# Shifting the slices of the transposed activations by 32 B each in a hybrid decoder layer

## The chip, the core and the metric

The kernel runs on one core of a Trainium2 chip. The metric is the device time of one execution in microseconds (us), median of the runs. The core's engines are called as in the profile: PE (TensorE, matmuls), PEld (its weight loads), DVE (VectorE), ACT (ScalarE), POOL (GpSimd) and SP (whose queue issues most transfers).

## The reference

One decoder layer on 256 tokens of 2048 features, all in float32. Two groups of attention heads share one input projection, one output projection follows, and then a gated feed-forward layer with a short causal convolution. Cut to what matters here:

```
h = rmsnorm(x, pre_mix_g)
proj = h @ w_in                       # 2048 -> 4368 columns: q, k, v of both groups, forget gates
o_a = sliding-window attention with sinks and ALiBi   (16 heads, 2 key/value heads)
o_b = forgetting attention with per-head gates        (16 heads)
x = x + rmsnorm(concat(rmsnorm(o_a), rmsnorm(o_b)) @ w_out, post_mix_g)
h = rmsnorm(x, pre_ffn_g)
u = causal_dwconv(h @ w_up)           # 2048 -> 11264 columns, width 3
gate, val = split(u)
x = x + rmsnorm((gelu(gate) * val) @ w_down, post_ffn_g)
```

## The kernel before

Every product is made from float32 operands that are split in two: a rounded high part and the rest, the low part. A product a*b is then taken as high*high + high*low + low*high. The tile hT holds the transposed normalised activations in this form: 16 slices (`kt`, one for each 128 of the 2048 features), and in each slice, for every one of 128 partitions, 256 high parts (one per token) and behind them 256 low parts, 512 float32 in all, which is 2048 B. The slices lie one behind the other, so that each begins at a multiple of 512 B. hT is filled from transposed x by ACT (high parts, L194) and DVE (low parts, L196) before the input projection, and a second time, as hT2, by L768 and L773 before the feed-forward layer. Then the same room serves once more, as `rest`, for some split weights of the last down projection.

Weights come in units of 1024 columns by SP's queue into `raw`, ACT rounds them into `whi`, and DVE writes the difference into `wlo` (L112 and L115). Where `still` is set, the low parts begin LOW = 56 elements, 224 B, into their buffer; whi and the unshifted wlo begin at multiples of 512 B.

The matmuls that read hT as the moving operand come in two kinds, with two output banks (m = 0, 1) for the two halves of 256 output columns:

```
pe.matmul(b, parts[u][0][:, a, m * P:(m + 1) * P], hT[:, kt, :], ...)                   # high
pe.matmul(b[:, 256:512], parts[u][1][:, a, m * P:(m + 1) * P], hT[:, kt, 0:256], ...)   # low
```

A high streams the 512 elements of a slice past 128 columns of whi, a low the first 256 past 128 columns of wlo. `proj_T4` (L284 and L290) serves the up projection: highs of slices 0 to 7 (16 matmuls), lows of 0 to 7, lows of 8 to 15, highs of 8 to 15, so that between groups of columns 32 highs or 32 lows follow each other. `proj_T` (L253 and L258) serves the queries and keys with stretches of 14 to 16, `unit_T` (L221 and L226) the first two groups, and `first_gate` (L928 and L932) the first columns of the up projection, half a slice at a time. In the value projection `mm3` (L309) uses hT the other way round: 128 elements of a slice are the weights, and 384 or 272 columns of whi and wlo stream.

PE's order is the order of the program text. The instructions of the other engines are ordered by a scheduler, except where the text fixes their order. Each matmul has a weight load of its own, which runs beside the matmul before it.

Matmuls that do not read hT: attention scores (L475), transposes of probabilities (L510), weighted sums (L522 to L536), output projection (`mm3` with oT), and the down projection (`product`, L967), where the weights are the moving operand and gated activations G or their sums are loaded.

The small tile gpre holds the gains of the first norm, 16 partitions of 512 B. It is loaded at L139 by ACT's queue, and read once, by the transpose at L175. The tile scr (tag "y") is scratch room for attention: rows and masks in its first 1280 columns, rotating scratch from column 1536 on, and from 1280 to 1536 the cumulated forget gates later on.

Of the kernel before, what the change touches and what calls it, by code (L numbers as in the profile page):

```python
# [8 lines left out]
F32 = mybir.dt.float32  # L9
F32R = mybir.dt.float32r  # L10
# [7 lines left out]
P = 128  # L18
S = 256
D = 2048  # L20
DFF = 5632
H = 16
KT = D // P
# [8 lines left out]
def hybrid_layer(ctx: ExitStack, tc: tile.TileContext, x, pre_mix_g, w_in, b_forget, sinks,  # L32
# [8 lines left out]
    const = ctx.enter_context(tc.tile_pool(name="const", bufs=1))  # L41
    main = ctx.enter_context(tc.tile_pool(name="main", bufs=1))
# [92 lines left out]
    const.tile([P, 120], F32, tag="room", name="room_c")  # L135
    small.tile([P, 112], F32, tag="room", bufs=1, name="room_s")

    gpre = const.tile([16, P], F32, tag="gpre", name="gpre")
    act.dma_start(gpre, pre_mix_g.rearrange("o (a p) -> (o a) p", p=P))  # L139
    x_in = main.tile([P, 2, D], F32, tag="x", name="x_in")  # L140
    xv = xf.rearrange("(t p) c -> p t c", p=P)

    first = [[], []]
# [1 line left out]
    for i in range(2):  # L145
        cs = slice(i * 256, (i + 1) * 256)
# [36 lines left out]
        pool.tensor_tensor(r, v, mhalf, op=ALU.pow)  # L183
        return r

    hT = main.tile([P, KT, 512], F32R, tag="hT", name="hT")
    def to_T(srcs, t0, n, g0, pin=False):

        for part in range(2):
            for kt, tb in srcs:  # L190
                hi = hT[:, kt, t0:t0 + n]
                gk = gcol[:, g0 + kt:g0 + kt + 1]
                if part == 0:
                    i = act.activation(hi, tb, AF.Copy, scale=gk)  # L194
                else:
                    i = dve.scalar_tensor_tensor(hT[:, kt, 256 + t0:256 + t0 + n], tb, gk,  # L196
                                                 hi.bitcast(F32), op0=ALU.mult, op1=ALU.subtract)
                if pin:
                    tc.keep_in_program_order(i)
# [115 lines left out]
    with tc.tile_pool(name="mixp", bufs=1) as mp:  # L315
# [30 lines left out]
                                   accum_out=sqx[t][:, c:c + 1]))  # L346


        scr = main.tile([P, 2 * D], F32, tag="y", name="scr")
        rowk, rowq, dist, u0, u1 = (scr[:, i * 256:(i + 1) * 256] for i in range(5))  # L350
        rot = [0]

# [278 lines left out]
        for p0, npair, cols in ((0, 3, 384), (3, 3, 384), (6, 2, 272)):  # L631
# [3 lines left out]
            for k0 in range(0, KT, per):  # L635
                na = min(per, KT - k0)
                hi, lo = w_unit(w_rows(w_in, k0, na, c0, cols), na, cols)
                for a in range(na):
                    kt = k0 + a
# [100 lines left out]
        out_half(1, evac_b, range(2))  # L740


        hT2 = main.tile([P, KT, 512], F32R, tag="hT", name="hT2")
        hT = hT2
        x_dram = tc.dram_tile([S, D], F32, name="x_dram")
        dffn, rmix = [], []
        sq2 = [small.tile([P, 4], F32, tag=f"sqm{t}", bufs=1, name=f"sqm{t}") for t in range(2)]
# [99 lines left out]
    with tc.tile_pool(name="ffn", bufs=1) as fp:  # L847
# [45 lines left out]
        def conv(b, ch, dst_tag):  # L893
            u = ubuf[cnt[0] % NU]
            cnt[0] += 1
            c = from_ring("cs")
            act.copy(c, b[:, 256:512])
            dve.tensor_tensor(u[:, 2:258], b[:, 0:256], c, op=ALU.add)  # L898
            pool.tensor_tensor(u[:, 2:258], u[:, 2:258], rowf, op=ALU.mult)  # L899
            y = from_ring(dst_tag)  # L900
            act.activation(y, u[:, 2:258], AF.Identity, bias=cw[:, 3, ch:ch + 1],  # L901
                           scale=cw[:, 2, ch:ch + 1])
            dve.scalar_tensor_tensor(y, u[:, 1:257], cw[:, 1, ch:ch + 1], y, op0=ALU.mult,  # L903
                                     op1=ALU.add)
            dve.scalar_tensor_tensor(y, u[:, 0:256], cw[:, 0, ch:ch + 1], y, op0=ALU.mult,
                                     op1=ALU.add)
            return y
# [141 lines left out]
        for half in range(2):  # L1049
# [4 lines left out]
            for g in range(FHALF // 2):  # L1054
# [11 lines left out]
                for m in range(2):  # L1066
                    y = conv(bg[m], c0 // P + m, "yg")
# [5 lines left out]
                for m in range(2):  # L1073
                    y = conv(bv[m], 44 + c0 // P + m, "yv")
# [90 lines left out]
        def rstd_y(t, n, v):  # L1165
            v2 = small.tile([P, 1], F32, tag="rv", name="rv")
            dve.scalar_tensor_tensor(v2, ysq[t][:, n:n + 1], 1.0 / D, v, op0=ALU.mult, op1=ALU.add)
            r = small.tile([P, 1], F32, tag="ry", bufs=2, name="ry")
            pool.tensor_tensor(r, v2, mhalf, op=ALU.pow)
            return r  # L1170
# [23 lines left out]
        r = rstd_y(0, 3, v)  # L1194
# [18 lines left out]
        r = rstd_y(1, 4, v)  # L1213
# [33 lines left out]
```

## Time and profile before

| | |
|---|---|
| median of 3 runs | 1064.84 us (1064.18 to 1065.08) |
| profiled execution, first to last instruction | 1062.6 us |
| instructions | 16272, of these 5890 matmuls |
| mean granted clock of TensorE | 0.996 |
| read from HBM | 201.68 MB, 194 GB/s over the span |

The profiled execution's own time is given as its span, from the first to the last instruction; the median of the runs lies 2.2 us above it. In the profile, L12 is line 12 of the kernel, `out<-in` are the program's names of what an instruction writes and reads, x counts instructions, and the records of successive matmuls overlap, so that the interval from one to the next is shorter than the duration of one. The chain of work is followed back from the last instruction, at each step to what released it.

### The profile page before, as it was taken

The numbers are of one execution on the slowest core, as the hardware profiler recorded it, in microseconds if no ns is written. First come the engines' busy times: TensorE is split into PE (matmuls) and PEld (weight loads), VectorE is DVE, ScalarE is ACT, GpSimd is POOL, SyncE is SP. The second block draws the span as 40 slices with busy tenths as digits, with TensorE's granted clock in tenths as the row PEclk, the third lists the DMA queues.
The fourth block names the chain that finished last, engine by engine and source line by source line (L and its number), as shares of the span: only waits on it lengthen the run. The fifth ranks groups of instructions, "written<-read, shape, count | busy, mean of one in ns | idle before, by whom it ended". The sixth has DMA issues, their size and how long they took to land.

```text
span 1062.6 us, 16272 instructions
## 1 busy us (share of the span) xinstructions
PE 1049.6 (99%) x5890; PEld 914.6 (86%) x5890; DVE 839.7 (79%) x1369; ACT 639.1 (60%) x1096; POOL 229.3 (22%) x256
## 2 busy tenths in 40 slices
PE   9999999999999999999999999999999999999996
PEld 7889988888889888888888888888888888888885
DVE  5988887887467887787767999668778687789987
ACT  6767667776556765566655556446556565556551
POOL 4253335441022121211212000002121121200004
PEclk9999999999999999999999999999999999999998
DMA  8745566555773876656665666666566665656563
GB/s 280 217 120 168 162 209 202 165 170 162 282 236 107 280 231 187 193 180 185 211 188 188 193 204 206 213 196 190 169 209 188 197 197 180 194 179 200 194 242 121
DMA packets 154285, 207.08 MB, mean 195 GB/s; under 512 B 6845, under 2 KB 131037, under 8 KB 153181
## 3 DMA queue, kind: packets, MB, share of 16 engines
q1 hardware_dynamic: 153200, 203.37, 60.7%
q10 hardware_dynamic: 1004, 2.68, 0.6%
q8 instruction: 46, 0.75, 0.3%
q14 instruction: 35, 0.28, 0.1%
HBM read 201.68 MB, written 4.21 MB: 194 GB/s over the span
## 4 chain that ended last, share of the span: by engine, by line
PE 84%; DVE 9%; issue 2%; DMA 2%; ACT 2%; POOL 1%; DVEq 0%; SPq 0%; POOLq 0%; ACTq 0%
PE bank_acc L284 15%; PE bank_att L284 14%; PE bank_acc L309 12%; PE bank_att L967 9%; PE bank_acc L290 8%; PE bank_att L290 7%; PE bank_acc L253 7%; DVE wlo L313 4%; PE bank_acc L258 4%; PE bank_acc L967 2%; PE bank_att L475 1%; PE bank_att L510 1%; DVE wlo L115 1%; PE bank_acc L932 1%; DMA raw<-in_w_down_dram 1%
## 5 line engine op out<-in xcount | busy, mean ns | idle before, releaser
L115 DVE TENSOR_TENSOR wlo<-raw,whi 128x1024 fp32r<-128x1024 f32 (+3 forms) x271 | 328.5, 1224 | 127.0 <-ACT whi L112 118.4
L112 ACT CAST whi<-raw 128x1024 fp32r<-128x1024 f32 (+3 forms) x270 | 273.2, 1029 | 131.8 <-issue 88.8
L899 POOL TENSOR_TENSOR room<-room,rowf 128x256 f32<-128x256 f32 x88 | 100.3, 1160 | 393.9 <-DVE room L898 392.0
L284 PE MATMUL bank_acc<-hT,whi 128*128 128x512 f32 x736 | 173.3, 390 | 0.0
L284 PEld LDWEIGHTS bank_acc<-hT,whi 128*128 128x128 f32 x736 | 136.4, 188 | 27.4
L967 PE MATMUL bank_att<-whi,G 128*128 128x512 f32 x488 | 156.0, 389 | 0.0
L284 PE MATMUL bank_att<-hT,whi 128*128 128x512 f32 x640 | 150.6, 390 | 0.0
L284 PEld LDWEIGHTS bank_att<-hT,whi 128*128 128x128 f32 x640 | 118.7, 188 | 23.9
L967 PEld LDWEIGHTS bank_att<-whi,G 128*128 128x128 f32 x488 | 91.6, 188 | 18.9
L967 PE MATMUL bank_att<-wlo,G 128*128 128x512 f32 x244 | 95.0, 389 | 0.2 <-DVE wlo L313 0.2
L290 PEld LDWEIGHTS bank_acc<-hT,wlo 128*128 128x128 f32 x736 | 89.3, 188 | 2.0
L290 PE MATMUL bank_acc<-hT,wlo 128*128 128x256 f32 x736 | 89.8, 279 | 0.0
L901 ACT ACTIVATE room<-room,cw 128x256 f32<-128x256 f32 x88 | 53.0, 602 | 60.6 <-POOL room L899 60.6
L253 PE MATMUL bank_acc<-hT,whi 128*128 128x512 f32 x352 | 88.0, 395 | 0.0
L309 PE MATMUL bank_acc<-whi,oT 128*128 128x512 f32 (+1 forms) x272 | 81.7, 379 | 0.0
L290 PEld LDWEIGHTS bank_att<-hT,wlo 128*128 128x128 f32 x640 | 77.6, 188 | 1.7
L290 PE MATMUL bank_att<-hT,wlo 128*128 128x256 f32 x640 | 77.9, 279 | 0.0
L903 DVE SCALAR_TENSOR_TENSOR room<-room,cw 128x256 f32<-128x256 f32 x88 | 62.4, 709 | 17.6 <-ACT room L901 17.3
L253 PEld LDWEIGHTS bank_acc<-hT,whi 128*128 128x128 f32 x352 | 63.3, 188 | 11.5
L313 DVE TENSOR_TENSOR wlo<-raw,whi 128x1024 fp32r<-128x1024 f32 (+1 forms) x56 | 61.3, 1119 | 12.1 <-ACT whi L312 12.1
L312 ACT CAST whi<-tb 128x1024 fp32r<-128x1024 f32 x42 | 44.0, 1050 | 43.0 <-PE bank_att L967 19.6
L312 ACT CAST whi<-raw 128x1024 fp32r<-128x1024 f32 (+1 forms) x56 | 52.3, 958 | 27.1 <-PE bank_att L967 20.6
(254 smaller groups left out, 1594.0 us busy)
## 6 DMA issues: line engine op xcount, KB each, us to landing
raw<-in_w_up_dram SPq DMA_DIRECT2D x176, 512.0 KB, 4.2
raw<-in_w_down_dram SPq DMA_DIRECT2D x58, 512.0 KB, 4.7
raw<-in_w_in_dram SPq DMA_DIRECT2D x51, 512.0 KB, 4.7
raw<-in_w_out_dram SPq DMA_DIRECT2D x32, 512.0 KB, 4.6
extra<-in_w_down_dram SPq DMA_DIRECT2D x20, 512.0 KB, 4.7
raw<-in_w_in_dram SPq DMA_DIRECT2D x16, 384.0 KB, 3.6
tb<-in_w_down_dram SPq DMA_DIRECT2D x10, 512.0 KB, 3.5
cb<-c_dram SPq DMA_DIRECT2D x8, 256.0 KB, 3.8
```

What stands on the lines that cost most here:

```text
L112: i1 = act.copy(hi[:, cs], raw[:, cs])
L115: i2 = dve.tensor_tensor(lo[:, cs], raw[:, cs], hi[:, cs].bitcast(F32), op=ALU.subtract)
L253: pe.matmul(b, parts[u][0][:, a, m * P:(m + 1) * P], hT[:, kt, :], start=(kt == 0), stop=(kt == KT - 1))
L284: pe.matmul(b, parts[u][0][:, a, m * P:(m + 1) * P], hT[:, kt, :], start=(kt == 0), stop=(kt == KT - 1))
L290: pe.matmul(b[:, 256:512], parts[u][1][:, a, m * P:(m + 1) * P], hT[:, kt, 0:256], start=False, stop=False)
L309: pe.matmul(b, a, r[:, cols], start=(first and i == 0), stop=(last and i == 2))
L312: act.copy(hi, src)
L313: dve.tensor_tensor(lo, src, hi.bitcast(F32), op=ALU.subtract)
L899: pool.tensor_tensor(u[:, 2:258], u[:, 2:258], rowf, op=ALU.mult)
L901: act.activation(y, u[:, 2:258], AF.Identity, bias=cw[:, 3, ch:ch + 1], scale=cw[:, 2, ch:ch + 1])
L903: dve.scalar_tensor_tensor(y, u[:, 1:257], cw[:, 1, ch:ch + 1], y, op0=ALU.mult, op1=ALU.add)
L967: pe.matmul(b[:, to] if to else b, a, r[:, cols], start=(first and i == 0), stop=(last and i == 2))
```

## The change

Slice k of hT now begins 512 + 8 elements, 2080 B, behind slice k - 1, so 32*k B past a multiple of 512. A class Rows stands for the tile and keeps the way in which the code indexes it. The tile grows by 512 B a partition; for that room gpre loses its own tile, and lies in scr[0:16, 1280:1408] instead. x_in, hT and scr are allocated earlier in the text, in the same order as before.

```
-    gpre = const.tile([16, P], F32, tag="gpre", name="gpre")
+    x_in = main.tile([P, 2, D], F32, tag="x", name="x_in")
+    SKEW = 8
+    class Rows:
+        def __init__(self, name):
+            self.t = main.tile([P, KT * (512 + SKEW)], F32R, tag="hT", name=name)
+        def __getitem__(self, at):
+            _, kt, cs = at
+            r = self.t[:, kt * (512 + SKEW):kt * (512 + SKEW) + 512]
+            return r[:, cs]
+    hT = Rows("hT")
+    scr = main.tile([P, 2 * D], F32, tag="y", name="scr")
+    gpre = scr[0:16, 1280:1408]
     act.dma_start(gpre, pre_mix_g.rearrange("o (a p) -> (o a) p", p=P))
-    x_in = main.tile([P, 2, D], F32, tag="x", name="x_in")
...
-    hT = main.tile([P, KT, 512], F32R, tag="hT", name="hT")
...
-        scr = main.tile([P, 2 * D], F32, tag="y", name="scr")
...
-        hT2 = main.tile([P, KT, 512], F32R, tag="hT", name="hT2")
-        hT = hT2
+        hT = Rows("hT2")
```

## The prediction

> **What bounds the kernel now.** I read the page first (busy shares, granted clock, the chain by line), then what TensorE waits for, then the chain of work in order of time, which gives the pace of each stretch of matmuls.
>
> ```profile
> PE 1049.6 (99%) x5890; PEld 914.6 (86%) x5890; DVE 839.7 (79%) x1369; ACT 639.1 (60%) x1096; POOL 229.3 (22%) x256
> PEclk9999999999999999999999999999999999999998
> PE 84%; DVE 9%; issue 2%; DMA 2%; ACT 2%; POOL 1%; DVEq 0%; SPq 0%; POOLq 0%; ACTq 0%
> ```
>
> TensorE is busy for 1049.6 of 1062.6 us, its granted clock is at the top digit until the last slice, and 84% of the chain is PE. The waits of PE are next; the columns are who waited for whom, us in total, times, longest us.
>
> ```profile
> PE bank_acc L169 <- DVE junk L164: 1.3, 1, 1.3
> PE bank_att L522 <- DVE pl L313: 0.5, 1, 0.5
> PE bank_acc L334 <- DMA x_in<-in_x_dram: 0.4, 1, 0.4
> PE bank_att L967 <- DVE wlo L313: 0.2, 1, 0.2
> ```
>
> These four are all that the view lists, 2.4 us together. So no other engine and no transfer holds PE up for long: whatever the change does to the interval from one matmul to the next goes straight into the time, and what it does on other engines does not, as long as they stay behind that little waiting. The matmuls that read hT are these (groups by line; after the count, busy us and mean ns of one record):
>
> ```profile
> L284 PE MATMUL bank_acc<-hT,whi 128*128 128x512 f32 x736 | 173.3, 390 | 0.0
> L284 PE MATMUL bank_att<-hT,whi 128*128 128x512 f32 x640 | 150.6, 390 | 0.0
> L290 PE MATMUL bank_acc<-hT,wlo 128*128 128x256 f32 x736 | 89.8, 279 | 0.0
> L290 PE MATMUL bank_att<-hT,wlo 128*128 128x256 f32 x640 | 77.9, 279 | 0.0
> L253 PE MATMUL bank_acc<-hT,whi 128*128 128x512 f32 x352 | 88.0, 395 | 0.0
> L258 PE MATMUL bank_acc<-hT,wlo 128*128 128x256 f32 x352 | 46.8, 281 | 0.0
> L309 PE MATMUL bank_acc<-whi,hT 128*128 128x384 f32 (+1 forms) x192 | 46.6, 322 | 0.0
> L309 PE MATMUL bank_acc<-wlo,hT 128*128 128x384 f32 (+1 forms) x96 | 30.6, 319 | 0.0
> ```
>
> That is 1376 + 352 = 1728 "highs" (512 columns of a slice, weights from whi), 1728 "lows" (256 columns, weights from wlo, which start 224 B past a multiple of 512), and 288 matmuls of the value projection, where hT is the weight and not the moving operand. The records overlap, so the 390 ns is no interval. The interval is read from the chain in order of time (start us, us, what, count):
>
> ```profile
> 455.55 7.29 PE bank_att L284 x32
> 462.84 3.73 PE bank_att L290 x32
> 466.57 3.65 PE bank_att L284 x16
> 470.22 3.63 PE bank_acc L284 x16
> ```
>
> A high takes 7.29/32 = 227.8 ns and a low 3.73/32 = 116.6 ns. The 16 highs just behind the lows take 3.65 us and the next 16 take 3.63. The timeline, cut at a start of such a stretch, shows why (start us, us from the first start to the last end):
>
> ```profile
> 521.51 1.32 PE L284 MATMUL bank_acc<-hT,whi 128*128 128x512 f32 x5
> 522.21 6.52 PE L284 MATMUL bank_acc<-hT,whi 128*128 128x512 f32 x28
> ```
>
> With 0.39 us for the last record, the first five highs start (1.32 - 0.39)/4 = 232.5 ns apart, the 28 from the fourth on (6.52 - 0.39)/27 = 227.0 ns. Nobody waits there: the same instruction on the same data layout is slow for some five matmuls after the switch from lows to highs, and then settles at 227 and stays. The pace is a steady state that has to be reached.
>
> **What the change does.** It adds and removes no instruction, semaphore or byte of transfer. It moves addresses: slice k of hT begins 2080 B behind slice k-1 instead of 2048, that is 32*k B past a multiple of 512. The weights do not move, so the distance (modulo 512 B) from the weights that are being loaded to the columns that stream past is no longer the same for all 16 slices, but goes round by 32 B a slice. In the loops a slice serves two matmuls (one per bank), so the distance changes at every second matmul. It also reads gpre from a corner of scr, and shifts what lies below hT by 512 B, which keeps its place modulo 512.
>
> The last part costs nothing:
>
> ```profile
> L139 ACTq DMA_DIRECT2D gpre<-in_pre_mix_g_dram x1: 458/458/458, 0.8 to 0.8; - x1
> L175 PE MATMUL bank_att<-ident,gpre x1: 283/283/283, 3.9 to 3.9; 16*128 16x16 f32 x1
> ```
>
> gpre is loaded at 0.8 us from ACT's queue and read once at 3.9 us, by L175. The columns of scr that it takes are written next by the cumulative sum of the forget gates, after the whole value projection; that stretch covers it, and without it one transpose of 0.283 us would be waited for. The writes of hT by ACT and DVE keep their shapes; at 32 B steps I put them at nothing too, since PE does not wait for ACT or DVE in the rows above beyond 0.7 us.
>
> What remains is what a changed distance does to an interval. The trace of before has three distances. Highs have distance 0 (slice and weights both at multiples of 512), lows 224. Two more stretches of the chain:
>
> ```profile
> 326.78 2.88 PE bank_acc L309 x24
> 234.61 0.69 PE bank_att L534 x3
> 235.31 0.36 PE bank_att L536 x3
> ```
>
> The 24 matmuls of 256 columns in the output projection have distance 0, and take 2.88/24 = 120.0 ns, against 116.6 for the lows: same width, no wait in either, other distance. So the distance matters, by 3.4 ns. The weighted sums L534 and L536 stream probabilities that lie 128 B past a multiple of 512 past weights at a multiple: 0.69/3 = 230 ns for 512 columns, 0.36/3 = 120 for 256.
>
> SBUF — State Buffer, section Who interferes with whom, of the Trainium skill gives PE two independent read ports, one for the moving operand and one for weights, and says "PE and ACT never wait on anyone"; by that the addresses would not matter and the sum would be zero. This trace differs from it by those 3.4 ns.
>
> **Highs.** Their interval at distance 0 is 227.0 settled and 232.5 unsettled; at 128 it is 230 in a run too short to settle. No row of 512 columns at another distance than 0 shows less than 227. If the distance changes at every second matmul and a run needs five to settle, the highs stay unsettled: between 230 and 232.5, and I take 231.5, nearer the row of the same loop. That is 231.5 - 227.8 = 3.7 ns, by 1728: 6.4 us. Bounds: at the lower end the 3.4 ns of gain that the lows have over distance 0, at the upper 232.5, 4.7 ns.
>
> **Lows.** They now have one fixed distance, and it is the better of the two that I can compare at this width: 116.6 at 224 against 120.0 at 0 and at 128. Going through all 16 they cannot keep it. I take the middle, 118.3, so 1.7 ns by 1728: 2.9 us. Bounds: nothing, and 3.4 ns (5.9 us).
>
> **Value projection.** Here the weights move and the stream stays.
>
> ```profile
> 74.44 7.31 PE bank_acc L309 x42
> ```
>
> 7.31/42 = 174.0 ns for 384 columns at distance 0. If it lost what I give the highs, 288 by 3.7 is 1.1 us; a slice serves six matmuls here, enough to settle in part, so 0.5, between 0 and 1.4 (4.7 ns by 288).
>
> **Sum.** 6.4 + 2.9 + 0.5 = 9.8 us, all on PE and all on the path. The profiled execution has a span of 1062.6 us and becomes 1072.4; the median of the runs is 1064.84, 2.2 us above that span, so the forecast is 1074.6. With the upper bounds it is 8.1 + 5.9 + 1.4 = 15.4, or 1080.2. The attention, the output and down projections and the tail keep their addresses modulo 512 and their times.
>
> **Rivals.** First, faster: the common distance 0 is what costs the highs, and breaking it helps them as the 224 B help the lows. Then 15 of 16 slices leave distance 0 and their highs gain 3.4 ns: 1728 x 15/16 x 3.4 = 5.5 us. The lows lose at the one slice of 16 that now meets them at distance 0 (k = 7, 32 x 7 = 224), 108 x 3.4 = 0.4 us. That gives 1064.8 - 5.5 + 0.4 = 1059.7. For it: 120.0 against 116.6 at 256 columns, the only comparison in which each side is a long run. Against it: 230 ns at distance 128, and that the settled state of highs is the lowest interval that I see for their width. It decides where the mean high falls below 227.8 by more than the 1.7 ns that I give the lows, that is at 226.1 or less.
>
> Second, no change: distance matters only for a narrow set of positions, or the pace settles anew within a pair of matmuls, and gains and losses cancel: within 2.1 us of 1064.8. For it: both widths have their slowest and fastest rows only 3 to 6 ns apart. Against it: each switch costs five matmuls of settling, and the new layout switches at every second one. The rule of the Trainium skill (SBUF — State Buffer, Who interferes with whom) would end here as well; the 3.4 ns speak against it as a reason.
>
> That the change does not do what it says would need the base of hT off a multiple of 512. That matters little: 16 slices at 32 B steps cover all positions wherever they begin.
>
> **How the numbers follow.** I give the forecast 0.6, faster 0.28, no change 0.12. 0.2% (2.1 us) is about what a measurement of this kernel can tell from no change; the forecast's own range, 1068 to 1080, lies above it and the faster rival's 1059.7 below, so the chances are these three. The eight-in-ten range must reach into the faster case: 1058 (the rival, and lows that gain a little too) to 1081 (the upper bounds, rounded up).
>
> **What would show it.** In the chain of the changed kernel, a stretch of 32 highs should take 32 x 231.5 = 7.41 us instead of 7.29 and 32 lows 32 x 118.3 = 3.79 instead of 3.73. The timeline inside a stretch should show no settling to 227. The waits of PE and the chain's stretches of L967, which read no hT, should be as before. I am wrong in the main step if highs settle anyway or run below 227.8, and in the second if lows stay at 116.6.

## The result, and the profile after

The changed kernel takes 1075.39 us (median of 4 runs, 1074.52 to 1076.08), the kernel before 1064.65 beside it (4 runs, 1064.18 to 1065.08): a ratio of 1.0102, with an interval of 1.0088 to 1.0116. The profiled execution of the changed kernel took 1075.15 us with a span of 1073.4, 10.8 more than the span before. The forecast was 1074.6, with a span of 1072.4.

In the changed kernel the lines stand 12 to 15 further down: L284 is now L298, L290 is L304, L253 is L267, L258 is L272, the matmul of `mm3` (L309) is L323 and that of `product` (L967) is L979. The page of the changed kernel:

```profile
PE 1058.9 (99%) x5890; PEld 915.4 (85%) x5890; DVE 837.7 (78%) x1369; ACT 639.3 (60%) x1096; POOL 230.1 (21%) x256
PEclk9999999999999999999999999999999999999998
PE 89%; DVE 6%; DMA 2%; issue 1%; ACT 1%; POOL 0%; SPq 0%; DVEq 0%; POOLq 0%; ACTq 0%
```

Same instructions, same granted clock, and PE busy for 9.3 us more. What PE waits for (who for whom, us in total, times, longest us):

```profile
PE bank_acc L184 <- DVE junk L179: 1.3, 1, 1.3
PE bank_att L979 <- DVE wlo L327: 1.0, 2, 0.5
PE bank_acc L348 <- DMA x_in<-in_x_dram: 0.7, 1, 0.7
PE bank_att L535 <- DVE pl L327: 0.5, 1, 0.5
PE bank_att L235 <- ACT whi L112: 0.4, 1, 0.4
```

That is 3.9 us against 2.4: no wait has grown to anything like the 10.8 us. The groups that read hT (count, busy us, mean ns of one record):

```profile
L298 PE MATMUL bank_acc<-hT,whi 128*128 128x512 f32 x736 | 176.7, 394 | 0.0
L298 PE MATMUL bank_att<-hT,whi 128*128 128x512 f32 x640 | 153.6, 394 | 0.0
L304 PE MATMUL bank_acc<-hT,wlo 128*128 128x256 f32 x736 | 91.2, 281 | 0.0
L304 PE MATMUL bank_att<-hT,wlo 128*128 128x256 f32 x640 | 79.1, 281 | 0.0
L267 PE MATMUL bank_acc<-hT,whi 128*128 128x512 f32 x352 | 89.0, 397 | 0.0
L272 PE MATMUL bank_acc<-hT,wlo 128*128 128x256 f32 x352 | 47.2, 283 | 0.0
L323 PE MATMUL bank_acc<-whi,hT 128*128 128x384 f32 (+1 forms) x192 | 46.8, 324 | 0.0
L323 PE MATMUL bank_acc<-wlo,hT 128*128 128x384 f32 (+1 forms) x96 | 30.8, 321 | 0.0
```

Set against the same rows of before, in busy us: highs of L298 3.4 + 3.0 more and of L267 1.0 more, 7.4 together; lows 1.4 + 1.2 + 0.4 = 3.0 more; the value projection 0.2 + 0.2 = 0.4 more. The sum is 10.8, the whole difference of the spans. Elsewhere PE waits 1.5 us longer, and the matmuls of the first two groups (L235 and L240, before L221 and L226) are 1.6 us less busy, so that the rest cancels. The chain in order of time and, below it, the timeline inside one stretch of highs (start us, us, what):

```profile
458.03 7.43 PE bank_att L298 x32
465.46 3.80 PE bank_att L304 x32
```

```profile
457.87 1.55 PE L298 MATMUL bank_att<-hT,whi 128*128 128x512 f32 x6
458.80 6.66 PE L298 MATMUL bank_att<-hT,whi 128*128 128x512 f32 x28
```

A high takes 7.43/32 = 232.2 ns (227.8 before), a low 3.80/32 = 118.8 (116.6 before). In the timeline, with about 0.39 us for the last record, the first six highs start 232 ns apart and the 28 that end the stretch (6.66 - 0.39)/27 = 232.2: the step down to 227, which the kernel before showed after five matmuls, does not come.

### The profile page after: what moved, and what is told of

Read it like the earlier page. It is cut to its first block, busy times and chain, and to the rows that moved or that the text cites. A ratio compares the mean times of both kernels' runs of the same rounds, so it can differ in the third digit from the quotient of the medians.

```text
span 1073.4 us, 16272 instructions
## 1 busy us (share of the span) xinstructions
PE 1058.9 (99%) x5890; PEld 915.4 (85%) x5890; DVE 837.7 (78%) x1369; ACT 639.3 (60%) x1096; POOL 230.1 (21%) x256
## 4 chain that ended last, share of the span: by engine, by line
PE 89%; DVE 6%; DMA 2%; issue 1%; ACT 1%; POOL 0%; SPq 0%; DVEq 0%; POOLq 0%; ACTq 0%
PE bank_acc L298 16%; PE bank_att L298 14%; PE bank_acc L323 12%; PE bank_att L979 11%; PE bank_acc L304 8%; PE bank_acc L267 7%; PE bank_att L304 7%; PE bank_acc L272 4%; PE bank_acc L979 3%; DVE wlo L327 2%; PE bank_att L488 1%; PE bank_att L523 1%; PE bank_acc L944 1%; PE bank_acc L235 1%; DMA tb<-in_w_down_dram 1%
## 5 line engine op out<-in xcount | busy, mean ns | idle before, releaser
L298 PE MATMUL bank_acc<-hT,whi 128*128 128x512 f32 x736 | 176.7, 394 | 0.0
L298 PEld LDWEIGHTS bank_acc<-hT,whi 128*128 128x128 f32 x736 | 136.5, 188 | 30.8
L979 PE MATMUL bank_att<-whi,G 128*128 128x512 f32 x488 | 156.1, 389 | 0.0
L298 PE MATMUL bank_att<-hT,whi 128*128 128x512 f32 x640 | 153.6, 394 | 0.0
L298 PEld LDWEIGHTS bank_att<-hT,whi 128*128 128x128 f32 x640 | 118.7, 188 | 26.8
L979 PEld LDWEIGHTS bank_att<-whi,G 128*128 128x128 f32 x488 | 91.6, 188 | 19.1
L979 PE MATMUL bank_att<-wlo,G 128*128 128x512 f32 x244 | 95.2, 390 | 1.0 <-DVE wlo L327 1.0
L304 PEld LDWEIGHTS bank_acc<-hT,wlo 128*128 128x128 f32 x736 | 90.5, 188 | 2.1
L304 PE MATMUL bank_acc<-hT,wlo 128*128 128x256 f32 x736 | 91.2, 281 | 0.0
L267 PE MATMUL bank_acc<-hT,whi 128*128 128x512 f32 x352 | 89.0, 397 | 0.0
L323 PE MATMUL bank_acc<-whi,oT 128*128 128x512 f32 (+1 forms) x272 | 81.8, 379 | 0.0
L304 PEld LDWEIGHTS bank_att<-hT,wlo 128*128 128x128 f32 x640 | 78.7, 188 | 1.8
L304 PE MATMUL bank_att<-hT,wlo 128*128 128x256 f32 x640 | 79.1, 281 | 0.0
L267 PEld LDWEIGHTS bank_acc<-hT,whi 128*128 128x128 f32 x352 | 63.4, 188 | 12.4
```

The source lines that it names most:

```text
L323: pe.matmul(b, a, r[:, cols], start=(first and i == 0), stop=(last and i == 2))
L979: pe.matmul(b[:, to] if to else b, a, r[:, cols], start=(first and i == 0), stop=(last and i == 2))
```

## The experiments

**The theories.** A is the prediction's: the pace of highs has to settle, a constant distance lets it settle, and a distance that changes at every second matmul keeps it from doing so. B: each distance has a price of its own, distance 0 is the cheap one for 512 columns, and how often the distance changes matters little. C: the price lies in the rest of the change (the class, gpre in scr, other allocations). All kernels of this part up to the map are the changed kernel with another address for slice `kt`:

```
-            r = self.t[:, kt * (512 + SKEW):kt * (512 + SKEW) + 512]
+            c = kt * 512 + 0        # e1; e2: + 8; e3: + 56; e4: + kt // 8 * 64; e9: + 34
+            r = self.t[:, c:c + 512]
```

**e1, all of the change but the shift** (slices 2048 B apart again).

> Everything of the change but the shift: the class Rows, the larger tile, gpre in scr, and slices 2048 B apart again. Theory A (the pace of the highs has to settle, and a distance from weights to slice that changes at every second matmul keeps it from settling) and theory B (each distance has its own price, whatever came before, and 0 is a cheap one) both expect the time of before, 1064.65 us within 1 us, with 7.29 us for 32 highs and 3.73 for 32 lows. Theory C (it is the rest: gpre, the 512 B shift of what lies below hT, another order of allocation) expects 1075 us.

Measured: 1064.11 us (1063.44 to 1065.42) against 1064.42, ratio 0.9996 (0.9987 to 1.0006). The chain of e1, where highs are L299 and lows L305, a line further down than in the changed kernel:

```profile
701.43 7.29 PE bank_acc L299 x32
708.71 3.73 PE bank_acc L305 x32
```

Highs and lows are back at the times of before. C falls, and the prediction's zero for gpre, the allocations and the room holds.

**e2 and e3, one constant shift for all slices**: 32 B, and 224 B. The distance no longer changes, so A lets the highs settle.

> All 16 slices 32 B past a multiple of 512 B, 2048 B apart: one fixed distance, another than before. Theory A: the highs settle again, at a level that I don't know but below 229.5 ns (32 highs in 7.34 us or less), the lows at a fixed distance of 192 B take 113 to 120 ns; 1060 to 1070 us. Theory B: the highs pay what the changed kernel shows on average at this distance, 233.9 ns (7.48 us for 32), the lows 117.3; 1064.65 + 1728 x 6.1 ns + 1728 x 0.6 ns = 1076 us.

> All slices 224 B past a multiple of 512 B, as the low weights are: the lows now have distance 0, the highs 288. Theory A: the lows settle at the 120.0 ns that 256 columns show at distance 0 (3.84 us for 32; 1728 x 3.3 ns = +5.7 us), the highs settle below 229.5 ns; about 1070 us, between 1065 and 1073. Theory B: by the averages of the changed kernel 235.3 ns for highs and 118.9 for lows, 1064.65 + 13.0 + 3.8 = 1081 us.

Measured: 1075.95 us and 1077.25 us (one run each; 1064.42 for the kernel before, whose 13 runs beside them lie between 1063.15 and 1066.21). The chain of e2, then that of e3:

```profile
706.68 7.46 PE bank_acc L299 x32
714.14 3.77 PE bank_acc L305 x32
```

```profile
705.55 3.82 PE bank_acc L305 x32
709.37 7.46 PE bank_acc L299 x32
```

Highs take 7.46/32 = 233.1 ns in both, more than in the changed kernel, though the distance is the same from one matmul to the next. e2 comes out where B put it, and e3 nearer to B's time than to A's. A's main step falls: a constant distance does not bring 227 back. In e3 the lows stand at distance 0 and take 119.4 ns, close to the 120.0 that the prediction read from the output projection.

**e4, slices 8 to 15 shifted by 256 B**, slices 0 to 7 not.

> Slices 0 to 7 at multiples of 512 B, slices 8 to 15 256 B past them: two distances, but each holds for 16 matmuls in a row. Theory A: highs settle within each run of 16; 32 highs take 7.29 to 7.40 us, 1064.5 to 1069 us. Theory B: half of the highs at distance 256 (231.7 ns), half of the lows at 480 (120.2): 1064.65 + 864 x 3.9 ns + 864 x 3.5 ns = 1071 us.

Measured: 1064.5 us (one run). The chain of e4:

```profile
702.10 7.29 PE bank_acc L299 x32
709.38 3.73 PE bank_acc L305 x32
```

Nothing at all is lost at 256 B. That was in A's range and not in B's, as B had then no reason to treat 256 B as 0. The map that follows gives the reason.

**e5, a map of the highs and lows with TensorE alone.** Series of 48 matmuls at one constant shift each, in steps of 32 B up to 512, and then series of 96 in which the shift grows by 32 B after 1, 2, 4, 8, 16 or 32 matmuls, and in one (`both`) slice and weights move on together (the loops around these lines are left out, here and below):

```
m0 = (i // 2) % 7 * 512 + moved(i) // 4
w0 = i % 8 * P + weights(i) // 4
pe.matmul(banks[i % 2][:, 0:n], whi[:, w0:w0 + P], hT[:, m0:m0 + n], ...)
...
run(f"H{d}_", 48, 512, moved=lambda i: d)
run(f"L{d}_", 48, 256, weights=lambda i: d)
run(f"hold{h}_", 96, 512, moved=lambda i: i // h * 32 % 512)
run("both_", 96, 512, moved=lambda i: i // 2 * 32 % 512, weights=lambda i: i // 2 * 32 % 512)
```

> Not the layer at all: it leaves out the whole computation and writes x as its output. TensorE alone runs series of matmuls on the first columns of x and w_in, one weight load for each, with nothing else on the chip. Series H0 to H480: 48 highs (512 columns) at one fixed offset of the slice, 0 to 480 B; L0 to L480: 48 lows (256 columns) at one fixed offset of the weights. Series hold1 to hold32: 96 highs whose offset moves on by 32 B after every 1, 2, 4, 8, 16 or 32 matmuls. Series both: slice and weights move on together by 32 B after every second matmul, so that the distance stays 0. Series same: 96 highs at 0; lows and lows2: 96 lows at a distance of 224 B, and the same with slices that move on by 32 B. Theory A: H0 and same at 227 ns; the other H series each settle at a level of their own, most of them below 230; hold1 and hold2 231 to 233 ns, falling towards the settled levels from hold4 to hold32; both at 227; lows 116.7 and lows2 118.6. Theory B: H32 to H480 at 231 to 235 ns each, hold1 to hold32 all alike at about 232. If it is the address itself and not the distance, both is as slow as hold2.

The timeline of e5 at the first matmul of the series at 0, 32, 64, 256 and 288 B (start us, us of that record; the digits are a part of the name):

```profile
26.18 0.39 PE L58 MATMUL H__115<-hT,whi 128*128 128x512 f32 x1
37.06 0.40 PE L58 MATMUL H__165<-hT,whi 128*128 128x512 f32 x1
48.26 0.40 PE L58 MATMUL H__215<-hT,whi 128*128 128x512 f32 x1
...
115.29 0.40 PE L58 MATMUL H__515<-hT,whi 128*128 128x512 f32 x1
126.18 0.40 PE L58 MATMUL H__565<-hT,whi 128*128 128x512 f32 x1
```

From one start to the next are 48 intervals: (37.06 - 26.18)/48 = 226.7 ns at 0, 233.3 at 32, and 226.9 at 256. Worked out in the same way from the trace, each the mean of two shifts, in ns:

| shift, B | 0, 256 | 32, 288 | 64, 320 | 96, 352 | 128, 384 | 160, 416 | 192, 448 | 224, 480 |
|---|---|---|---|---|---|---|---|---|
| highs (slice shifted) | 226.8 | 233.4 | 229.1 | 233.5 | 233.3 | 234.2 | 233.2 | 233.1 |
| lows (weights shifted) | 119.7 | 118.2 | 117.9 | 117.4 | 118.5 | 119.8 | 117.7 | 118.0 |

The second half repeats the first: the price goes by the distance modulo 256 B, not 512, which is why e4 lost nothing. And how long a shift is held hardly matters for the mean: the highs take 234.0, 232.4, 232.2, 232.2 and 232.1 ns when it moves after 1, 2, 4, 8 and 16 matmuls. (After 32 the series reaches only 0, 32 and 64 B, and takes 230.0.) The sixteen slices of the changed kernel go through the eight columns of the table twice; their mean is 232.1 ns, against 232.2 in the chain of the changed kernel. Slice by slice the two do not agree, so that a part of this is cancellation: in the trace of the changed kernel, slice 0 (0 B) takes 231.6 ns from one start to the next, where the map has 226.8, and slices 4 and 12 (128 B) take 232.0, where it has 233.3. No other engine works in e5 while PE does, so the price is not one of contention with other engines.

One series went against both theories. In `both`, slice and weights move on together by 32 B at every second matmul, and A and B alike put it at 227; to be as slow as hold2 (232.4) was set down as the sign that the address itself has the price. The first matmuls of `both` and of the series behind it:

```profile
429.05 0.40 PE L58 MATMUL both__2303<-hT,whi 128*128 128x512 f32 x1
451.39 0.40 PE L58 MATMUL same__2401<-hT,whi 128*128 128x512 f32 x1
```

That is (451.39 - 429.05)/96 = 232.7 ns, as slow as hold2. e6 separates address and distance.

**e6, finer steps, and the parts of the distance one by one** (H, L: the map in steps of 8 B; W: only the weights shifted; E: both shifted alike, by a constant amount; A: the slice's shift changing at every second matmul).

```
+run(at("H", i), 40, 512, moved=lambda n: i * 8)
+run(at("L", i), 40, 256, weights=lambda n: i * 8)
+run(at("W", i), 40, 512, weights=lambda n: i * 32)
+run(at("E", i), 40, 512, moved=lambda n: i * 32, weights=lambda n: i * 32)
+run(at("A", i), 96, 512, moved=lambda n: n // 2 % 2 * i * 32)
```

> TensorE alone; it leaves out the whole computation and writes x as its output. Series of 40 matmuls, each with a weight load of its own, seven slices of 512 columns in turn. H: highs (512 columns), slice shifted by 0, 8, 16 ... 248 B. L: lows (256 columns), weights shifted by the same steps. W: highs, the weights shifted by 0, 32 ... 224 B and the slice not. E: highs, slice and weights both shifted by the same 32 ... 224 B. A: 96 highs, the slice's shift going between 0 and 32, 64, 128 or 256 B after every second matmul. Theory B (each distance from weights to slice, modulo 256 B, has its price, whatever the addresses themselves are): E at 226.7 ns throughout; W at 233 to 234 except 226.7 at 0 and about 229 at the shift of 192, where the distance is 64; H between its neighbours of the 32 B steps; A at 0/256 at 226.7, at 0/32 and 0/128 at 232 to 233, at 0/64 between 229 and 232. Rival, the slice's own address has the price: W at 226.7 throughout, E as H (233 to 234, 229 at 64). Theory A, what is left of it (a change of distance by itself costs the settled pace): A at 0/256 at 231 to 233 as well. Lows: 117 to 120 at every shift by B; a finer step that is under 116.6 would be the first gain to be had.

The chain of e6 (the two letters number the shift: aa is 0, ae 32 B, ba 64 for H; bd is 88 and cf 168 for L; ag 192 for W; ah 224 for E; ab is 0 and 32 in turn, ba 0 and 256 in turn, for A):

```profile
25.79 9.07 PE Haa L58 x40
62.84 9.34 PE Hae L58 x40
100.16 9.17 PE Hba L58 x40
376.15 4.55 PE Lbd L58 x40
423.60 4.56 PE Lcf L58 x40
531.09 9.17 PE Wag L58 x40
604.20 9.10 PE Eah L58 x40
613.30 22.30 PE Aab L58 x96
679.92 21.77 PE Aba L58 x96
```

Shifting slice and weights together leaves the highs at 9.10/40 = 227.5 ns, the first few slow ones included, where shifting the slice alone by as much costs 233. Weights shifted by 192 B give 229.2, as slices shifted by 64 do. So here the distance counts, with its sign, and not the slice's own address. Alternating between 0 and 256 B costs nothing (226.8); alternating between 0 and 32, 64 or 128 B takes 232.3, 230.0 and 231.7, where the means of the two prices are 230.1, 228.0 and 230.1. About 2 ns are left of A: a distance of 0 that is held for two matmuls doesn't get its cheap pace. That may be what slows `both` as well, since each weight load runs beside the matmul before: where the two move on together, the weights being loaded are already 32 B ahead of the slice that still streams. No run tests this. The lows have places at 113.8 and 114.0 ns, at 88 and 168 B, under the 116.6 of the kernel before and under the 117 to 120 that B expected at every shift. At 224 B they take 116.8 here, where the series of e5 had 118.0 at the same addresses.

**e7, the odd steps of 4 B.** The same kernel with shifts of 4, 12, ... 252 B, and with 384 columns (M) and alternating lows (Q) in place of W, E and A.

```
-run(at("H", i), 40, 512, moved=lambda n: i * 8)
-run(at("L", i), 40, 256, weights=lambda n: i * 8)
+run(at("H", i), 40, 512, moved=lambda n: i * 8 + 4)
+run(at("L", i), 40, 256, weights=lambda n: i * 8 + 4)
+run(at("M", i), 40, 384, weights=lambda n: i * 8)
+run(at("Q", i), 96, 256, weights=lambda n: n // 2 % 2 * i * 8)
```

> TensorE alone; it leaves out the whole computation and writes x as its output. H: highs (512 columns), slice shifted by 4, 12, 20 ... 252 B. L: lows (256 columns), weights shifted by the same. M: 384 columns, weights shifted by 0, 8 ... 248 B. Q: 96 lows, the weights' shift going between 0 and 88 B, and between 0 and 168 B, after every second matmul. Theory B: the odd steps lie among their neighbours, highs 227 to 236 ns and lows 113 to 120; 384 columns at 173.3 at 0 and 174 to 180 elsewhere; Q between 113.4 and 120 and nearer the upper, as the cheap pace at 88 and 168 B has to be held. A high under 226.7 at any step would be a gain that no kernel here has.

The chain of e7 at 60 and 132 B for the highs, at 204 B for the lows, and at 0 for 384 columns:

```profile
91.80 9.14 PE Hah L58 x40
175.82 9.59 PE Hca L58 x40
443.75 4.54 PE Ldb L58 x40
476.97 6.94 PE Maa L58 x40
```

Measured: highs at these steps lie between 228.7 (at 60 B) and 239.8 ns, most neighbouring steps 5 to 10 ns apart, which is up to 4 ns over what was expected. With e6 that makes 64 positions, and none has a high under 226.7. Lows reach 113.5 to 113.8 at 52, 76 and 204 B. 384 columns are at about 173.4 at 0 and at a dozen other steps, and at most 179.5. Going between 0 and 88 B gives the lows 118.2, nearer the upper price as expected; between 0 and 168 B they take 116.8, the mean of the two.

**e8, e9 and e11, the map put to use.** e8 and e11 are the kernel before with another `LOW`; e9 is the changed kernel with all slices at 136 B, so that lows stand at 224 - 136 = 88 B and highs at 136.

```
-    LOW = 56
+    LOW = 22        # e8 at 88 B; 42: e8 at 168 B; 51: e11 at 204 B
```

> The kernel before, with the low parts of the weights 88 B instead of 224 B into their buffer. If the map of distances carries over (theory B): 32 lows in 3.63 to 3.65 us instead of 3.73, 1728 lows gain 3 ns each, 5 us, and the highs stay at 7.29: 1059 to 1060.5. Rival, the price is not one of the distance but of this kernel's stretches (short ones lose the cheap pace at each switch from highs to lows): 1063 to 1065, lows at 116 or more.

> The kernel before, with the low parts 168 B into their buffer, the other cheap distance of the map. Theory B: as at 88 B, 1059 to 1060.5, 32 lows in 3.63 to 3.65 us. Rival: 1063 to 1065.

> The changed kernel, but with every slice 136 B past a multiple of 512 and none of the going round, so that the distance of the lows is 88 B and that of the highs 136 B. Theory B prices the two apart: 32 highs in 7.46 to 7.47 us (233.5 ns each, 9.8 us more in all), 32 lows in 3.63 to 3.65 us (5 us less): 1069 to 1070. Rival, any slice off a multiple of 256 B slows both kinds, as both constant shifts tried so far did: 1075 to 1077.

> The kernel before, with the low parts of the weights 204 B into their buffer, where a series of lows ran at 113.3 ns from its first matmul on. If that holds in the whole kernel: 32 lows in 3.63 us, and the stretches of queries and keys gain as well: 1058 to 1060. If the stretch before decides and highs at distance 0 lead to the other pace: 32 lows in 3.80 to 3.84, 1066 to 1068.

A stretch of 32 lows in the chains of e8 at 88 B, e8 at 168 B, e9 and e11:

```profile
706.05 3.65 PE bank_acc L290 x32
```

```profile
710.57 3.84 PE bank_acc L290 x32
```

```profile
718.15 3.82 PE bank_acc L305 x32
```

```profile
714.29 3.94 PE bank_acc L290 x32
```

| kernel | us | ratio to before (interval) | a low, ns |
|---|---|---|---|
| e8, 88 B | 1059.97 | 0.9954 (0.9941 to 0.9966) | 114.1 |
| e8, 168 B | 1067.99 | 1.0033 (1.0021 to 1.0045) | 120.0 |
| e9 | 1078.39 | 1.0130 (1.0116 to 1.0143) | 119.4 |
| e11, 204 B | 1074.35 | 1.0090 (1.0073 to 1.0107) | 123.1 |

One of the four came out as the map said: at 88 B the lows gain 2.5 ns, 1728 x 2.5 = 4.3 of the 4.8 us measured, and the kernel is faster than both kernels of this case. In the other three the lows miss the series by 6 to 10 ns, at the distances 168, 88 and 204 B, where long series had 114.0, 113.8 and 113.5. In e9 the rival's time, 1075 to 1077, was the nearer one; at 168 and at 204 B the kernel is slower than both times set down for it. So B is incomplete for lows: one distance can have more than one steady pace.

**e10, the kernels' own stretches with TensorE alone**: twelve cases, each four times 32 highs and then 32 lows.

```
+run("highs_" + case, 32, 512, moved=lambda n: high)
+run("lows_" + case, 32, 256, moved=lambda n: low[0], weights=lambda n: low[1])
```

> TensorE alone; it leaves out the whole computation and writes x as its output. Twelve cases, each four times 32 highs and 32 lows in turn. The lows at distance 88 B took 113.5 ns when the slices lay at multiples of 512 B, and 120 when slices lay 136 B further and the highs before them ran at 233.5. Cases: a, highs at distance 0, slice 0 and low weights 88; b, highs with the slice at 136, lows with slice 136 and weights 224; c, highs as in a and lows as in b; d, highs as in b and lows as in a. If a distance has several steady paces and the stretch before decides which is reached: a and c 32 lows in 3.63 to 3.65 us, b and d 3.80 to 3.84. If the addresses themselves count and not only their distance: a and d 3.63 to 3.65, b and c 3.80 to 3.84. Further: e, lows at 168 after highs at distance 0 (3.84 as in the whole kernel, though 113.4 ns was measured at 168 in a long series); f, lows at 224 (3.73 to 3.77); g and h, lows at 88 after highs at 32 and 64 B (open which pace); i and j, lows at 204 after highs at 32 B and at 0 (3.63 in both, as 204 was at 113.3 from its first matmul on); k and l, lows at distance 0 after highs at 0 and at 32 B (3.80 to 3.84).

The chain of e10, one pass of case a, the lows of c and d, and the lows of i in its second and third pass:

```profile
37.64 7.28 PE highs_a L58 x32
44.91 3.65 PE lows_a L58 x32
122.91 3.82 PE lows_c L58 x32
167.47 3.63 PE lows_d L58 x32
400.07 3.83 PE lows_i L58 x32
411.37 3.63 PE lows_i L58 x32
```

Lows take 3.82 in b and c and 3.63 to 3.65 in a and d, all at distance 88 B. The highs ahead of them differ within each pair, so here the addresses count and not the stretch before: slices and weights 136 B further on are dearer at the same distance. (The E series of e6 were moved by multiples of 32 B, and lost nothing.) But the addresses do not settle it either. In case i, which was expected at 3.63 throughout, the third pass finds 113.4 ns and the other three 119.4 or more, at the same addresses and behind the same highs; e (168 B) takes 3.84 = 120.0 ns a low where the series of e6 had 114.0, and j (204 B) 3.94 = 123.1 where that of e7 had 113.5. Of the others, g and h (88 B behind highs at 32 and 64 B) take 3.66, and k and l (distance 0) 3.82 to 3.84. What e10 does give is the time in the whole kernel: a 3.65, e 3.84, j 3.94, f (224 B) 3.73 and b 3.82 us equal the stretches of e8 at 88 B, e8 at 168 B, e11, the kernel before, and e9, to the hundredth. So the lows' other paces too arise in TensorE's own work, with no other engine in it.

## Why the prediction came out, point by point

**That PE bounds the kernel, and the rest is worth nothing**: right. e1 has everything but the shift and is at 0.9996. (That PE waits for ACT or DVE no longer than 0.7 us was misread: the rows have 1.3 us more for DVE's junk, ahead of the first matmul, which has nothing to do with hT.)

**Highs, 6.4 us**: the direction was right and the term a little small, 7.4 us by the groups. The prediction took 231.5 ns between 230 and 232.5, "nearer the row of the same loop"; the chain has 232.2. This 1.0 us is the distance between the forecast span of 1072.4 and the 1073.4 measured.

**The reason for them failed in its main step**: "the distance changes at every second matmul and a run needs five to settle, the highs stay unsettled". e2 and e3 don't change the distance and are as slow. In place of the step stands a price for each distance modulo 256 B, where it is held: 227 at 0, 229 at 64, 233 to 234 at the other six steps of 32 B. Of the settling there remains that distance 0 has to be held for its 227 (0 and 32 B in turn: 232.3; slice 0 of the changed kernel: 231.6). So the size of the term came out well by luck: 231.5 was taken from an unsettled pace, and the mean of the prices happens to lie beside it, at 232.1. The sign that the prediction set for being wrong here, highs that settle or run below 227.8, did not appear, because a price for each distance keeps the highs slow as well; it took a constant shift, as in e2, to tell the two apart. The trace of before could not show the prices, as its long stretches of highs all had distance 0.

**Lows, 2.9 us**: right at 3.0. They had a better place than the mean at 224 B and lost it, as the prediction said. Its size was the middle of two rows, 118.3, and the mean of the eight columns of the map is 118.4 (the chain: 118.8).

**Value projection, 0.5 us**: 0.4 by the groups. The stretch that the prediction quoted, 7.31 us for 42 matmuls, is now 73.52 to 80.87:

```profile
73.52 7.35 PE bank_acc L323 x42
```

**The faster rival** took the 3.4 ns between two rows of 256 columns over to 512. The map shows where that fails: with 256 columns distance 0 is among the two dearest of the eight steps, with 512 it is the cheapest. **The rival of no change** needed gains and losses to cancel; both widths lost. The rule that the prediction weighed there, two independent read ports of PE (the Trainium skill, SBUF — State Buffer, Who interferes with whom), does not foresee the result. e5, in which PE works alone, has 226.8 and 233.4 ns for the same instruction with a slice shifted by 32 B.

**Open**: what in the chip makes the price; why 256 B; why a distance that alternates costs some 2 ns more than the mean of its prices, and whether this is what slows `both`; why 136 B under both operands changes the pace of lows; and what decides between two paces at the same addresses. That two reads of PE meet in the memory is a guess that fits the distance, and nothing here shows it.

## What to carry to other kernels

Where PE is the bound, the place of the weights being loaded against the columns that stream is a setting like any other: in the whole kernels here, 6 ns of 228 hung on it for highs, and 9 of 114 for lows. A spread of addresses came out near the mean of the places instead of the best, so choose one, for each width by itself. Time it with PE alone in the kernel's own succession of stretches, not in long series of one kind: for lows the first agreed to the hundredth of a microsecond in five layouts, the second was wrong in three of four.

## What the runs showed of the hardware

The interval of these matmuls, each with a weight load of its own, settles in short repeating patterns, often on one value: 113.3, 120, 173.3, 226.7, 233.3 or 240 ns, all whole multiples of 6.67 ns (17, 18, 26, 34, 35 and 36 times). At five of the eight steps of 32 B a high settles one such step above its best, at 233.3 against 226.7. Lows also settle between 113.3 and 120, in patterns whose mean is no such multiple (117.4 at 96 B). Their best, 113.3 ns, is half of the best high.
